# Hyena layer: two pieces of channels in flight, and the short convolution as scaled copies summed by accumulating DMAs

## The chip, the cores and the metric

The kernel runs on one core of a Trainium2 chip. The metric is the device time of one execution in microseconds, as the median of several runs. The five engines have a queue of instructions each, which they work off in order and which wait for one another by semaphores: TensorE (PE, with its weight loads as PEld), VectorE (DVE), ScalarE (ACT), GpSimd (POOL) and SyncE (SP). The last two also issue DMAs.

## The reference

An encoder trunk of two layers on 1024 tokens with 1024 channels: layer 0 mixes by attention and RWKV-7, layer 1 by an order-2 Hyena operator, and both end in a SwiGLU network. The change lies in layer 1's operator:

```
def hyena_mixer(h, w_in, conv_w, conv_b, ..., skip, w_out):
    p = h @ w_in                                  # 1024 -> 3072 channels
    p = conv(p, conv_w, width 3, centred, per channel) + conv_b
    v, x1, x2 = jnp.split(p, 3, axis=-1)
    filt = hyena_filters(...)
    z = v
    for o, gate in enumerate((x1, x2)):
        z = gate * bidirectional_fft_conv(z, filt[:, o, 0], filt[:, o, 1], skip[o])
    return z @ w_out
```

All is in fp32.

## The kernel before, in words

Everything in SBUF lives in pages of 128 partitions by 1024 floats, named `p` in the profile, handed out and taken back in turn; in PSUM there are eight banks (`bk`), in this layer four for the projection (group 0) and four for the convolutions (group 1). A page or bank that is handed out again makes its next writer wait for its last reader.

The projection `p = h @ w_in` makes 24 tiles of 128 channels: 8 for v, 8 for x1, 8 for x2. A tile is 48 matmuls (L296: three products of high and low parts, two halves of the tokens, eight blocks of input channels). The weights of a tile come in two DMAs from GpSimd's queue (L271, `hwi..h` and `hwi..l`), issued one tile ahead. ScalarE then empties the two banks into a padded page (`padded`, L1036), and `hy_short` forms the width-3 convolution: one scaled copy with bias on ScalarE (L1852) and two multiply-adds on VectorE (L1853, L1854). v and x1 tiles are transposed on TensorE (`hy_tok`, L1865) and copied back by ScalarE (L1866). x2 tiles are stored in DRAM (`sp_h`).

Channels are worked in four pieces q of 256, that is two tiles each of v, x1 and x2. Of a piece, `start` makes the first half of a DFT on TensorE (L1804, copied to SBUF at L1805). `hy_conv` does the rest on VectorE: `dft8` (L1654 and L1655), the product with the filter's spectrum, which comes by DMA from `hs` (L1827 to L1832), the first sums of the inverse (L1838, L1839) and another `dft8`. `gate` ends the inverse on TensorE (L1957), multiplies by x1 on VectorE (L1962) and begins the next DFT (`hy_taps`: L1814 on TensorE, L1704 on ScalarE, L1705 and L1706 on VectorE). A second `hy_conv` follows, and `finals` ends the inverse (L1980), multiplies by x2 (L1984) and stores the result (`sp_z`). The pieces run one after another. Under the name `tail` the first four results then go through the first half of the output projection (L256 and L257 split them into high and low parts, L296 multiplies, L787 adds to the residual). The second half (`halves`: L296, L814) follows the stage and ends in the norm before the SwiGLU network.

`weave` interleaves generators of such steps in proportion to quotas: here the chain of pieces (`back`) against the projection followed by `tail` (`rest`). The tile framework then schedules each engine's queue from that program order by its own estimates, so that the order on an engine can differ from that of the code.

Of the kernel before, what the change touches and what calls it, by code (L numbers as in the profile page):

```python
# [12 lines left out]
AF = mybir.ActivationFunctionType  # L13
ALU = mybir.AluOpType
# [7 lines left out]
P = 128  # L22
# [41 lines left out]
def run(gen):  # L64
    for _ in gen:
        pass
# [10 lines left out]
class Kern:  # L77
# [1766 lines left out]
        yield 2.2  # L1844
        return out

    def hy_short(self, pad, j):

        nc = self.nc
        o = self.page()  # L1850
        cw = lambda a: self.c("conv_w", 24 * a + j)
        nc.scalar.activation(out=o, in_=pad[:, 1:1025], func=AF.Identity, scale=cw(1), bias=self.c("conv_b", j))  # L1852
        nc.vector.scalar_tensor_tensor(out=o, in0=pad[:, 0:1024], scalar=cw(0), in1=o, op0=ALU.mult, op1=ALU.add)  # L1853
        nc.vector.scalar_tensor_tensor(out=o, in0=pad[:, 2:1026], scalar=cw(2), in1=o, op0=ALU.mult, op1=ALU.add)  # L1854
        self.free(pad)
        return o
# [13 lines left out]
    def hyena(self, w, h, tail):  # L1870
# [7 lines left out]
        zs = []  # L1878
# [47 lines left out]

        def there(q, n):
            while rs[q].get("n", 0) < n:
                yield

        def Bt(B, t2):
            j, s = self.xpos(t2)
# [3 lines left out]

        def start(q):

            if q < 4:
                yield from there(q, 2)  # L1940
                v = rs[q]["v"]
                st[q] = self.quads(4, 256)
                for t in range(4):
                    self.hy_sums(st[q], v, t, 1)
                    yield 0.1
                self.free(v)

        def gate(q, B):

            x1 = rs[q]["x1"]  # L1950
            s = self.quads(4, 256)
            for i in range(4):
                ps = self.bank(1, (P, 2, 256))
                for j in range(2):
                    t2 = i + 4 * j
                    for ri in range(2):
                        nc.tensor.matmul(ps[:, j], self.G[t2 // 4][:, t2 % 4, 128 * ri : 128 * ri + 128], Bt(B, t2)[:, ri], start=ri == 0, stop=ri == 1)  # L1957
                if i:
                    self.hy_taps(s, x1, i - 1, 1)
                for j in range(2):  # L1960
                    z = x1[j][:, i]
                    nc.vector.tensor_tensor(out=z, in0=z, in1=ps[:, j], op=ALU.mult)  # L1962
                self.fbank(ps)
                yield 0.1
            self.free(B[0])
            self.hy_taps(s, x1, 3, 1)
            self.free(x1)
            yield 0.1
            return s

        def finals(q, B):

            for c in range(2):
                x2 = self.unspill(rs[q]["x2", c])
                for i in range(2):
# [7 lines left out]
                    xv = x2.rearrange("p (a b) -> p b a", b=8)[:, 4 * i : 4 * i + 4]  # L1983
                    nc.vector.tensor_tensor(out=xv, in0=xv, in1=ps, op=ALU.mult)  # L1984
                    self.fbank(ps)
                zs.append(self.spill(x2, f"sp_z{2 * q + c}"))
                self.free(x2)
            self.free(B[0])

        def back():  # L1990
            yield from start(0)
            end = iter(())
            for q in range(4):
                steps = self.hy_conv(st.pop(q), 0, q)
                while True:
                    try:
                        cost = next(steps)
                    except StopIteration as e:
                        B = e.value
                        break  # L2000
                    next(end, None)
                    yield cost
                run(end)
                yield from there(q, 4)
                s = yield from gate(q, B)
                B = yield from self.hy_conv(s, 1, q, start(q + 1))
                yield from there(q, 6)
                end = finals(q, B)
            yield from end

        def rest():
            yield from f
            for a in h:
                self.free(a)
            while len(zs) < 4:
                yield
            for n, _ in enumerate(tail(zs[:4])):
# [7 lines left out]
        return zs[4:]  # L2025


    def final(self, xT, steps, out):
# [182 lines left out]
```

## Time and profile before

| | us |
|---|---|
| median of 3 runs | 3393.94 (3389.41 to 3398.52) |
| the profiled execution | 3396.35 |
| its span | 3394.6 |
| mean granted TensorE clock | 0.958 |
| TensorE busy over the span | 3177.3 (94%) |
| VectorE busy | 2343.3 (69%) |
| ScalarE busy | 1230.9 (36%) |
| GpSimd busy | 197.2 (6%) |

Rows of the profile give a line of the code, the engine, the operation with its tiles, and counts. A row of the order of time begins with start and length in us and ends, in brackets, with the idle time before it and what ended that. Busy time of a matmul includes its pipelined part, so that rows of TensorE overlap a little; the price of one is better taken from the starts of two rows. An fp32 matmul that is not split by the program counts as two instructions in the trace; L296 works on already split parts and counts once. The Hyena stage begins near 2105 us and its last product of a piece ends at 2649 us.

### The profile page before, as it was taken

The page shows a single profiled execution, that of the slowest core. Times are in us where ns is not written, and L with a number is a line of the kernel's source. Part 1 is how long each engine was busy: PE and PEld are TensorE (multiplying, and loading weights), DVE is VectorE, ACT ScalarE, POOL GpSimd, SP SyncE. Part 2 cuts the span into 40 slices and gives each one's busy share as a digit, 9 for nine tenths or more (in the row PEclk, how much of TensorE's full clock was granted, in tenths as well). Part 3 has the DMA queues.
Part 4 walks back from the last instruction along what each step waited for, and adds up shares of the span by engine and source line. Part 5 has one row for each costly group of instructions (what it writes and reads, how often), then busy time and mean ns, then how long its engine had stood idle before and what let it go on. Part 6 is the DMA issues. An engine that isn't in the chain of part 4 may idle for free.

```text
span 3394.6 us, 51189 instructions
## 1 busy us (share of the span) xinstructions
PE 3177.3 (94%) x20227; PEld 2565.5 (76%) x20227; DVE 2343.3 (69%) x4011; ACT 1230.9 (36%) x2146; POOL 197.2 (6%) x443
## 2 busy tenths in 40 slices
PE   8899989988889997999999999989977899999998
PEld 5687767666667886888888887877866788888886
DVE  5465465565766896788877666698997686667545
ACT  4622255455555432532323333222220343333211
POOL 2000000000001110000001210000000000000000
PEclk9999989889999998999999999999988899999999
DMA  7654522333334235244447993323445422224311
GB/s 265 222 174 153 153 71 67 66 98 66 102 68 103 86 137 185 93 158 140 148 148 249 351 317 131 118 89 110 143 167 208 145 81 75 75 93 148 122 47 50
DMA packets 331377, 460.24 MB, mean 136 GB/s; under 512 B 101816, under 2 KB 233745, under 8 KB 331136
## 3 DMA queue, kind: packets, MB, share of 16 engines
q1 hardware_dynamic: 292576, 322.04, 30.9%
q0 software_dynamic: 38384, 134.86, 11.3%
q8 instruction: 159, 2.61, 0.3%
q14 instruction: 82, 0.67, 0.1%
q10 hardware_dynamic: 176, 0.07, 0.0%
HBM read 312.71 MB, written 141.56 MB: 134 GB/s over the span
## 4 chain that ended last, share of the span: by engine, by line
PE 57%; DVE 7%; DMA 5%; issue 4%; ACT 2%; POOL 0%; DVEq 0%; SPq 0%; ACTq 0%; POOLq 0%
PE bk L296 20%; PE bk L600 8%; PE bk L602 8%; PE bk L601 8%; PE bk L1785 3%; DMA p<-in_hy_w_in_dram 2%; DVE p L1654 2%; PE bk L1804 2%; DVE p L257 1%; PE bk L1760 1%; PE bk L1980 1%; PE bk L1332 1%; PE bk L964 1%; PE bk L1814 1%; PE bk L947 1%
## 5 line engine op out<-in xcount | busy, mean ns | idle before, releaser
L296 PE MATMUL bk<-p,p 128*128 128x512 f32 x5136 | 1240.9, 401 | 65.9 <-ACT p L256 31.1
L296 PEld LDWEIGHTS bk<-p,p 128*128 128x128 f32 x5136 | 980.4, 193 | 289.4 <-ACT p L256 34.0
L256 ACT ACTIVATE p<-p 128x512 fp32r<-128x512 f32 (+3 forms) x542 | 403.2, 758 | 946.3 <-PE bk L601 271.2
L257 DVE TENSOR_TENSOR p<-p,p 128x512 fp32r<-128x512 f32 (+3 forms) x542 | 450.8, 847 | 238.7 <-ACT p L256 188.4
L601 PE MATMUL bk<-p,p 128*128 128x512 f32 x1248 | 486.1, 390 | 3.8 <-DVE p L257 3.8
L600 PE MATMUL bk<-p,p 128*128 128x512 f32 x1248 | 485.6, 390 | 0.0
L602 PE MATMUL bk<-p,p 128*128 128x512 f32 x1248 | 485.2, 390 | 0.2 <-DVE p L257 0.2
L601 PEld LDWEIGHTS bk<-p,p 128*128 128x128 f32 x1248 | 234.7, 188 | 53.1 <-DVE p L257 4.7
L602 PEld LDWEIGHTS bk<-p,p 128*128 128x128 f32 x1248 | 234.7, 188 | 49.6 <-DVE p L257 0.6
L600 PEld LDWEIGHTS bk<-p,p 128*128 128x128 f32 x1248 | 234.7, 188 | 48.1
L787 DVE SCALAR_TENSOR_TENSOR p<-bk,mod,p 128x512 f32<-128x512 f32 x192 | 134.8, 744 | 85.5 <-PE bk L296 82.0
L429 DVE SCALAR_TENSOR_TENSOR p<-p,cond,p 128x512 f32<-128x512 f32 x140 | 104.6, 749 | 58.8 <-DMA p<-in_ada_w_dram 56.7
L1785 PE MATMUL bk<-p,p 128*128 128x256 f32 x512 | 127.6, 397 | 6.0 <-DVE p L1706 4.9
L1654 DVE TENSOR_TENSOR p<-p 128x256 f32<-128x256 f32 (+1 forms) x336 | 130.8, 452 | 0.0
L1785 PEld LDWEIGHTS bk<-p,p 128*128 128x128 f32 x512 | 96.7, 197 | 21.0 <-DVE p L1706 6.0
L928 DVE TENSOR_REDUCE mx<-bk 128x1 f32<-128x512 f32 x128 | 86.5, 685 | 36.7 <-PE bk L925 34.8
L1036 ACT COPY p<-bk 128x512 f32<-128x512 f32 (+1 forms) x80 | 43.9, 588 | 182.9 <-DVE p L1831 63.0
L932 ACT ACTIVATE p<-bk,mx 128x512 f32<-128x512 f32 x128 | 87.0, 686 | 51.6 <-DVE mx L929 46.4
L1654 DVE TENSOR_TENSOR p<-p,p 128x1024 f32<-128x1024 f32 (+1 forms) x144 | 91.1, 681 | 18.8 <-ACT p L1805 18.8
L1332 PEld LDWEIGHTS bk<-p,p 64*64 64x64 f32 x2048 | 75.7, 141 | 37.0 <-issue 18.5
L1332 PE MATMUL bk<-p,p 64*64 64x64 f32 x2048 | 88.4, 230 | 16.0 <-DMA p<-o 8.6
L947 PE MATMUL bk<-k_ident,p 128*128 128x128 f32 x512 | 88.4, 302 | 15.5 <-ACT p L932 11.5
(407 smaller groups left out, 4169.9 us busy)
## 6 DMA issues: line engine op xcount, KB each, us to landing
p<-in_ffn_w_dram SPq DMA_DIRECT2D x120, 512.0 KB, 5.3
p<-in_ada_w_dram SPq DMA_DIRECT2D x96, 512.0 KB, 4.6
sp_f<-p POOLq DMA_DIRECT2D x36, 512.0 KB, 5.5
p<-sp_f POOLq DMA_DIRECT2D x36, 512.0 KB, 5.8
hs<-p POOLq DMA_DIRECT2D x32, 512.0 KB, 3.7
p<-hs SPq DMA_DIRECT2D x32, 512.0 KB, 4.5
p<-sp_r SPq DMA_DIRECT2D x24, 512.0 KB, 5.0
p<-sp_x SPq DMA_DIRECT2D x24, 512.0 KB, 4.6
```

What stands on the lines that cost most here:

```text
L256: self.nc.scalar.activation(out=hi, in_=src, func=AF.Copy)
L257: self.nc.vector.tensor_tensor(out=lo, in0=src, in1=hi.bitcast(F32), op=ALU.subtract)
L296: nc.tensor.matmul(ps[n], a, b[:, HALVES[n]], start=s, stop=e)
L429: nc.vector.scalar_tensor_tensor(out=acc, in0=wt[:, i], scalar=self.cond[:, k : k + 1], in1=acc, op0=ALU.mult, op1=ALU.add)
L600: nc.tensor.matmul(ps, op[:, 0, k], mh, start=start and k == 0, stop=False)
L601: nc.tensor.matmul(ps, op[:, 0, k], ml, start=False, stop=False)
L602: nc.tensor.matmul(ps, op[:, 1, k], mh, start=False, stop=stop and k == 3)
L787: nc.vector.scalar_tensor_tensor(out=xs, in0=ps[n], scalar=self.modc(layer, part, m), in1=xs, op0=ALU.mult, op1=ALU.add)
L947: nc.tensor.transpose(pt[:, j], pr[:, k * P : (k + 1) * P], self.ident)
L1332: nc.tensor.matmul(pt[H[p], pr], lhs(e, pr, p), rhs[H[p], 8 * e + pr], start=True, stop=True)
L1654: tt = lambda o, a, b, op: nc.vector.tensor_tensor(out=o, in0=a, in1=b, op=op)
L1785: nc.tensor.matmul(ps[j][:, ri], F[2 * d + t2 // 4][:, t2 % 4, 128 * ri : 128 * ri + 128], tp[:, j, d], start=d == 0, stop=d == 1)
```

## The change

Two things, in one diff.

First, of the 24 projected tiles the four v tiles of pieces 0 and 1 keep the old short convolution. For the other 20, ScalarE makes all three scaled copies, the two outer ones into pages of their own, and two DMAs on GpSimd's queue add these to the first (`accum_op=ALU.add`). The second must wait for the first, because both read and write the same page. The step after the convolution is asked for 8 steps of the projection later instead of 4.

Second, two pieces are in flight: one line of work takes pieces 0 and 2, the other 1 and 3, and both are woven with the projection. The tiles come in the order v, x1, x2 of pieces 0 and 1, then of 2 and 3. The token form of x1 is stored in DRAM (`sp_hx`) and loaded again at the gate. Final products no longer run inside the next piece's first convolution.

```diff
-    def hy_short(self, pad, j):
+    def hy_short(self, pad, j, by_dma):
...
         nc.scalar.activation(out=o, in_=pad[:, 1:1025], func=AF.Identity, scale=cw(1), bias=self.c("conv_b", j))
+        if by_dma:
+            for a in (0, 2):
+                s = self.page()
+                nc.scalar.activation(out=s, in_=pad[:, a : a + 1024], func=AF.Identity, scale=cw(a))
+                nc.gpsimd.dma_start(out=o, in_=s, accum_op=ALU.add)
+                self.free(s)
+            self.free(pad)
+            return o
         nc.vector.scalar_tensor_tensor(out=o, in0=pad[:, 0:1024], scalar=cw(0), in1=o, op0=ALU.mult, op1=ALU.add)
...
-        tiles = [(q, key, c, j + 2 * q + c) for q in range(4) for key, j in (("v", 0), ("x1", 8), ("x2", 16)) for c in range(2)]
+        tiles = [(q, key, c, j + 2 * q + c) for h2 in range(2) for key, j in (("v", 0), ("x1", 8), ("x2", 16)) for q in (2 * h2, 2 * h2 + 1) for c in range(2)]
...
-            o = self.hy_short(pad, j)
-            for _ in range(4):
+            by_dma = key != "v" or q > 1
+            o = self.hy_short(pad, j, by_dma)
+            for _ in range(8 if by_dma else 4):
                 yield
...
                 self.hy_tok(r[key], o, c)
+                if key == "x1" and c == 1:
+                    t = r[key]
+                    flat = lambda a: a.rearrange("p a b -> p (a b)")
+                    r[key] = [self.spill(flat(a), f"sp_hx{q}{n}") for n, a in enumerate(t)]
+                    self.free(t)
...
-            x1 = rs[q]["x1"]
+            x1 = [reshape(self.unspill(d), (P, 4, 256)) for d in rs[q]["x1"]]
...
-        def back():
-            yield from start(0)
...
+        def back(q):
+
+            yield from start(q)
+            B = yield from self.hy_conv(st.pop(q), 0, q)
+            yield from there(q, 4)
+            s = yield from gate(q, B)
+            B = yield from self.hy_conv(s, 1, q)
+            yield from there(q, 6)
+            yield from finals(q, B)
+
+        def line(h2):
+
+            for q in (h2, 2 + h2):
+                yield from back(q)
...
-        weave((335, back()), (267, rest()))
+        weave((168, line(0)), (168, line(1)), (300, rest()))
```

In the changed kernel lines from 1857 on have new numbers: the accumulating DMA is L1857, the two outer copies L1856, the multiply-adds L1861 and L1862, the transposes L1873 with their copies L1874, the gate's matmul L1970 and product L1975, the final matmul L1993 and product L1997. Lines before 1847 keep theirs.

How the queues change, at three places. On GpSimd's queue before, where the projection is at the first x1 tiles, there are only the weights of coming tiles and the zeros of the padded pages (L1033, L1034):

```order
L271 DMA p_238<-hwi10h 128x1024 [waits DMASW5_49,PE_49]
L271 DMA p_10858<-hwi10l 128x1024 [waits DMASW6_49,PE_49]
L271 DMA p_10846<-hwi11h 128x1024 [waits DMASW7_49,PE_49]
L271 DMA p_10874<-hwi11l 128x1024 [waits DMASW0_49,PE_49]
L1033 MEMSET p_16085 128x1 [waits DVE_49,Activation_49]
```

and now (`DMASW` is a wait for a DMA of this queue):

```order
L1857 DMA p_86<-p_106 128x1024 [waits DMAHW7_49,Activation_49]
L1033 MEMSET p_94 128x1 [waits Pool_49]
L1034 MEMSET p_94 128x1 [waits Activation_49]
L1857 DMA p_86<-p_126 128x1024 [waits DMASW7_49]
L1033 MEMSET p_16057 128x1 [waits DMAHW6_49,DVE_49]
L271 DMA p_10846<-hwi11h 128x1024 [waits DMASW3_49,PE_49]
L271 DMA p_10874<-hwi11l 128x1024 [waits DMASW4_49,PE_49]
```

Between two pairs of weights there now stands a pair of accumulations, of which the second waits for the first.

On SP's queue before, around the first gate, the spectra (`hs`, L1827) and the stores of x2 (`sp_h`) alternate, and x1 does not appear:

```order
L1827 DMA p_16041<-hs_9434 128x1024 [waits DVE_49,Activation_49]
L206 DMA sp_h_16683<-p_16053 128x1024 [waits DMASW2_49,DMAHW1_49,DVE_49,Activation_49]
L206 DMA sp_h_16772<-p_102 128x1024 [waits DMAHW2_49,DVE_49]
L1827 DMA p_106<-hs_10347 128x1024 [waits DMAHW6_49,DVE_49,PE_49]
L1827 DMA p_16041<-hs_10347 128x1024 [waits DMAHW0_49,DMAHW4_49,DVE_49,PE_49]
```

and now:

```order
L206 DMA sp_hx_16823<-p_16045 128x1024 [waits DMAHW4_49,Activation_49]
L206 DMA sp_hx_16825<-p_16081 128x1024 [waits DMAHW7_49,DMAHW5_49,Activation_49]
L1827 DMA p_16081<-hs_9720 128x1024 [waits DMAHW6_49,DMAHW5_49]
L206 DMA sp_h_17168<-p_86 128x1024 [waits DMASW0_49,Pool_49]
L211 DMA p_126<-sp_hx_16823 128x1024 [waits DMAHW4_49,DVE_49]
L211 DMA p_90<-sp_hx_16825 128x1024 [waits DMAHW1_49,DVE_49]
```

The loads of x1 for the first gate stand behind the store of the first x2 tile, which waits for that tile's accumulations.

On VectorE's queue before, behind the last gate, the spectral products of one piece follow one another (`L1838` and `L1839` are its next sums):

```order
L1831 TENSOR_TENSOR p_16061<-p_16053 128x2x256
L1832 TENSOR_TENSOR p_16061<-p_16045 128x2x256
L1831 TENSOR_TENSOR p_16069<-p_16057 128x2x256
L1832 TENSOR_TENSOR p_16069<-p_106 128x2x256
L1655 SCALAR_TENSOR_TENSOR p_130<-p_114,p_16077 128x256 x2
L1655 SCALAR_TENSOR_TENSOR p_94<-p_114,p_16077 128x512 x2
L1655 SCALAR_TENSOR_TENSOR p_130<-p_114,p_16077 128x256 x2
L1838 TENSOR_TENSOR p_90<-p_16061 128x512
```

and now:

```order
L1655 SCALAR_TENSOR_TENSOR p_130<-p_114,p_16057 128x256 x2
L1838 TENSOR_TENSOR p_16065<-p_16053 128x512
L1838 TENSOR_TENSOR p_102<-p_90 128x512
L1838 TENSOR_TENSOR p_102<-p_16073 128x512
L1839 TENSOR_TENSOR p_86<-p_16073 128x512
L1828 TENSOR_TENSOR p_16057<-p_16085,p_16069 128x512
L1828 TENSOR_TENSOR p_94<-p_16049,p_16081 128x512
L1829 TENSOR_TENSOR p_94<-p_16049,p_16081 128x512
L1829 TENSOR_TENSOR p_16057<-p_16085,p_16069 128x512
L1828 TENSOR_TENSOR p_16053<-p_130,p_16045 128x512
```

Sums of the one piece (L1838, L1839) now stand ahead of spectral products of the other (L1828, L1829): behind the last gate two pieces are on their way to the end.

More of the change, by code (lines that the diff above doesn't have):

```diff
@@ L1928, in there @@
             while rs[q].get("n", 0) < n:
-                yield
+                yield "wait"
         def Bt(B, t2):
@@ L1937, in start @@
         def start(q):
[L1939 to L1946, printed above, removed]
+            yield from there(q, 2)
+            v = rs[q]["v"]
+            st[q] = self.quads(4, 256)
+            for t in range(4):
+                self.hy_sums(st[q], v, t, 1)
+                yield 0.5
+            self.free(v)
         def gate(q, B):
-            x1 = rs[q]["x1"]
+            x1 = [reshape(self.unspill(d), (P, 4, 256)) for d in rs[q]["x1"]]
             s = self.quads(4, 256)
@@ L1985, in finals @@
                     self.fbank(ps)
-                zs.append(self.spill(x2, f"sp_z{2 * q + c}"))
+                zs[2 * q + c] = self.spill(x2, f"sp_z{2 * q + c}")
                 self.free(x2)
             self.free(B[0])
-        def back():
-            yield from start(0)
[L1992 to L2009, printed above, removed]
+        def back(q):
[9 more added lines that the diff above has]
+                yield from back(q)
         def rest():
@@ L2015, in rest @@
             while len(zs) < 4:
-                yield
-            for n, _ in enumerate(tail(zs[:4])):
+                yield "wait"
+            for n, _ in enumerate(tail([zs[i] for i in range(4)])):
                 yield 1.0 if n == 0 else 5.3
```

4 lines of the change are left out of this document (2 added, 2 removed).

## The prediction

> **What bounds the stage now.** I read the windows first, to see which engine carries the Hyena stage, then the chain of waits of TensorE inside it, then the order of time for the price of each kind of work. The span is 3394.6 us, the profiled execution 3396.35 us, 2.4 us above the median of the runs shown (3393.94), so I work in the trace and subtract 2.4 at the end.
>
> The windows, core 0: length, then busy time of TensorE, of its weight loads, of VectorE, ScalarE and GpSimd with instruction counts, then the granted clock, the DMA share and GB/s.
>
> ```profile
> 2108.70:2590.50 481.80, 443.31 (x2042) 371.51 (x2042) 402.88 (x695) 99.82 (x149) 29.26 (x78) 0.95 0.39 130
> 2594.50:2649.00 54.50, 29.75 (x121) 24.37 (x122) 51.28 (x92) 1.06 (x1) 3.18 (x6) 0.72 0.60 199
> 2296.00:2321.00 25.00, 25.00 (x112) 20.75 (x111) 24.96 (x41) 2.33 (x3) 2.41 (x7) 1.00 0.43 155
> ```
>
> From the third projection to the last gate, TensorE is busy 92% and VectorE 84%: both are near full, and neither alone sets the time. In the last 54.5 us VectorE is busy 94%, and TensorE waits at a clock of 0.72: there VectorE sets it.
>
> What TensorE waited for between 2108.7 and 2590.5 (total us, times, longest), then the rows at the borders of these windows:
>
> ```profile
> PE bk L1865 <- ACT p L1036: 16.9, 4, 5.8
> PE bk L296 <- ACT p L256: 12.4, 2, 7.9
> PE bk L296 <- ACT p L1866: 5.3, 3, 4.5
> PE bk L1814 <- DVE p L1706: 1.8, 3, 0.6
> PE bk L1814 <- DVE p L1962: 1.4, 1, 1.4
> PE bk L1804 <- ACT p L1866: 0.5, 2, 0.3
> ...
> 2108.70 8.95 PE L296 MATMUL bk<-p,p 128*128 128x512 f32 x27 [4.28 <-DMA p<-hwi8h]
> 2589.82 1.02 PE L1814 MATMUL bk<-p,p 128*128 128x256 f32 x4
> 2590.50 3.80 PE L296 MATMUL bk<-p,p 128*128 128x512 f32 x15
> 2593.89 0.68 DVE L1706 SCALAR_TENSOR_TENSOR p<-p,bk 128x512 f32<-128x512 f32 x1
> 2644.59 4.39 DVE L1984 TENSOR_TENSOR p<-p,bk 128x512 f32<-128x512 f32 x4 [3.17 <-PE bk L1980]
> ```
>
> The idle time is 481.8 - 443.3 = 38.5 us. The five rows other than L256 sum to 25.9: they lie around the gates, where one piece has nothing for VectorE until its gate is through. The L256 row (12.4) is the output projection that waits for the first pieces.
>
> **TensorE's floor.** Prices at full clock, from starts in the order of time:
>
> ```profile
> 2117.48 1.06 PE L1865 MATMUL bk<-k_ident,p 128*128 128x128 f32 x8
> 2118.30 10.50 PE L296 MATMUL bk<-p,p 128*128 128x512 f32 x45
> ...
> 2257.32 7.07 PE L1804 MATMUL bk<-p,p 128*128 128x256 f32 x32
> 2264.04 0.81 PE L296 MATMUL bk<-p,p 128*128 128x512 f32 x2
> ...
> 2281.20 5.52 PE L1980 MATMUL bk<-p,p 128*128 128x128 f32 x48
> 2286.56 0.27 PE L1865 MATMUL bk<-k_ident,p 128*128 128x128 f32 x1
> 2286.59 33.61 PE L296 MATMUL bk<-p,p 128*128 128x512 f32 x147
> 2320.04 1.89 PE L1957 MATMUL bk<-p,p 128*128 128x256 f32 x8
> 2321.58 4.94 PE L296 MATMUL bk<-p,p 128*128 128x512 f32 x20
> ```
>
> L296: 33.45/147 = 0.2276 us. L1804: 6.72/32 = 0.21. L1980: 5.36/48 = 0.1117. L1957: 1.54/8 = 0.1925, and L1814, of the same shape, alike. Transposes: 0.82/8 = 0.1025. An fp32 product counts as two instructions in the trace. Up to the last L1814, before issues 1209 L296, 128 transposes, 256 L1804, 128 each of L1957 and L1814, 192 L1980: 275.1 + 13.1 + 53.8 + 49.3 + 21.4 = 412.7. So 481.8 holds 69.1 beyond the floor: 38.5 idle and 30.6 of matmuls at less than full clock. After issues 1213 L296 and 128 L1980 there, the rest alike: 406.5.
>
> **The parts of the change.**
>
> *Short convolution of 20 tiles.* Forty VectorE operations go, forty ScalarE operations and forty DMAs on GpSimd's queue come:
>
> ```profile
> L1854 DVE SCALAR_TENSOR_TENSOR p<-p,cols,p x24: 1266/1277/1285, 2108.7 to 2532.9; 128x1024 f32<-128x1024 f32 x24
> L1852 ACT ACTIVATE p<-p,cols x24: 1237/1246/1262, 2105.0 to 2528.5; 128x1024 f32<-128x1024 f32 x24
> 2123.16 1.08 ACT L1036 COPY p<-bk 128x512 f32<-128x512 f32 x2 [3.96 <-PE bk L296]
> 2195.75 0.75 DVE L1962 TENSOR_TENSOR p<-p,bk 128x256 f32<-128x256 f32 x2 [0.38 <-PE bk L1957]
> 2303.04 0.53 POOL L271 DMA_DIRECT2D p<-hwi12h  x1 [9.81 <-PE bk L296]
> 2303.56 0.54 POOL L271 DMA_DIRECT2D p<-hwi12l  x1
> ```
>
> VectorE loses 40 x 1.28 = 51 us of 403. That is no gain by itself, because TensorE's 406.5 stand above it; it makes room for two pieces. ScalarE gains 40 x 1.25 = 50 on 99.8 in 481.8: hidden, at about a third busy. GpSimd's queue gains 40 x 0.53 = 21 on 29: hidden as issue time. Its waits are another matter: the second accumulation of a tile waits on that queue for the first, and the weight loads (L271) stand behind. A tile's projection is 48 L296, 11 us, and a load may be one tile late in the queue before TensorE misses it.
>
> *The latency D of an accumulating DMA* is not in this trace. The nearest rows:
>
> ```profile
> hs<-p POOLq DMA_DIRECT2D x32, 512.0 KB, 3.7
> sp_x<-p SPq DMA_DIRECT2D x16, 256.0 KB, 2.0
> sp_h<-p SPq DMA_DIRECT2D x8, 512.0 KB, 4.1
> p<-sp_h SPq DMA_DIRECT2D x8, 512.0 KB, 3.6
> hwi5l<-p POOLq DMA_DIRECT2D x1, 512.0 KB, 10.1
> ```
>
> If the extra read of the destination is free, D is 3.7. If it is serial, 512 KB more cost twice (4.1 - 2.0), so D is 7.9. Beside a crowd of transfers it is 10.1 + 4.2 = 14.3 at worst. I take 5.8, midway between the first two, since the stage's DMA share is only 0.39.
>
> How much may D be? The x1 loads of a gate stand on SP's queue behind the spill of the first x2 tile, which waits for both its accumulations. From the end of that tile's projection to the gate's first L1814 there stand on TensorE 71 L296 (16.2), 16 L1957 (3.1) and 16 transposes (1.6): 20.9 us. The path is 3.6 on ScalarE (both evacuations, 1.08, and two scaled copies of 1.25), 2D, 3.6 for the load and 0.7 for the products (L1962): it fits while D is under 6.5. Above that each us of D costs 2 us at each of four gates. At 5.8 it costs nothing.
>
> *Two pieces in flight.* The DVE order lets one piece's DFT and spectral products run while the other passes its gate, so part of the 25.9 us of waits goes. I take half, 13.0: with 51 us less on VectorE (about 330 us of work before the last gate instead of 403) either piece mostly has something ready, but ScalarE's evacuations still wait for pages that now also hang on DMAs. The L256 waits (12.4) go: at the projection's place all four first pieces have been stored long before. The slow-clock time I scale with the waits: 30.6 x 13.0/38.5 = 10.3. So up to the last gate: 406.5 + 13.0 + 10.3 = 429.8, against 481.8: **52.0 less.** What ends last there is TensorE's own queue.
>
> The start is as before: VectorE's first DFT waits for the first piece's 64 L1804, which stand at the same place. The new quotas of the weaving and the order of the 24 tiles act only through the order counted here.
>
> *x1 through DRAM* adds 8 stores and 8 loads of 512 KB on SP's queue. They are hidden (3.6 to 4.1 us each, DMA share 0.39) except through the path above.
>
> *The tail* gets longer, because two pieces now end together. Prices:
>
> ```profile
> 2619.14 1.28 DVE L1828 TENSOR_TENSOR p<-p,p 128x512 f32<-128x512 f32 x2
> 2621.55 1.40 DVE L787 SCALAR_TENSOR_TENSOR p<-bk,mod,p 128x512 f32<-128x512 f32 x2
> 2622.87 2.34 DVE L1830 TENSOR_TENSOR p<-p,p 128x1024 f32<-128x1024 f32 x2
> 2629.95 2.35 DVE L1654 TENSOR_TENSOR p<-p,p 128x1024 f32<-128x1024 f32 x2
> ...
> 2638.79 2.62 DVE L1655 SCALAR_TENSOR_TENSOR p<-p,p 128x256 f32<-128x256 f32 x6
> ```
>
> Behind the last gate VectorE has three DFTs instead of two, five spectral products instead of four, 13 sums instead of 8 and 8 final products instead of 4. A DFT is 2629.95 to 2641.41 = 11.46; a spectral product 4 x 0.64 + 1.17 = 3.73; five sums 3.2; four finals 4.4; two L787 and one L257 fewer save 1.4 + 1.2. That is 11.46 + 3.73 + 3.2 + 4.4 - 2.6 = **20.2 more**. TensorE has 33 L296 (7.5 us) to do there: no cover. The second half of the output projection then has 24 L296 behind the tail that stood in its waits before (5.5), and two more splits behind the last finals (L257, of L1830's size: 2 x 1.17 = 2.3): **7.8 more**.
>
> The sum: 52.0 - 20.2 - 7.8 = 24.0 less. 3396.35 - 24.0 = 3372.3, less 2.4: **3370 us**.
>
> **A rule that speaks against it.** The row at 2303.04 is a GpSimd DMA issue of 0.53 us inside a stretch in which VectorE was busy 24.96 of 25.00 us, and it was followed 0.52 us later by the next issue. The Trainium skill, page "SBUF — State Buffer", section "Who interferes with whom", says that a DMA issued by GpSimd can stall because a VectorE operation in a two-port mode keeps GpSimd from writing descriptors. By that rule forty more such DMAs beside a busy VectorE would be the new bottleneck; the trace speaks against it here, and the same page says that tensor_tensor has no such mode.
>
> **Rivals.**
>
> 1. *The gates' waits stay* (ScalarE's evacuation waits for a page, now of either piece). Then 25.9 idle and 30.6 x 25.9/38.5 = 20.6 slow clock remain: 453.0, 28.8 less, against 28.0 more behind it. 3393 us, no change. For it: the largest row, L1865 behind L1036, is such a wait. Against it: 51 us less on VectorE, which frees those pages.
> 2. *Accumulation latency on the gates' path: slower.* At D = 12 it costs 4 x 2 x (12 - 6.5) = 44: 3414 us. The gain is gone at 6.5 + 24/8 = 9.5. For it: the 10.1 row and in-order queues on SP, GpSimd and ScalarE. Against it: a free DMA share of 0.6.
> 3. *VectorE starves descriptor writing: slower.* If each of the 40 DMAs waited half of a 25 us stretch, 500 us would be added, near 3870. Nearly excluded by the issue row above.
> 4. *All waits and all slow clock go:* 406.5, so 75.3 less and 28.0 more: 3347 us.
>
> **Chances and range.** The forecast 0.53, rival 1 0.19, rival 2 and other slower mixes of it 0.21, rival 3 0.02, rival 4 0.05. The median's bound for telling a change is 0.3%, 10.2 us. Faster: 0.53 + 0.05 = 0.58, of which 0.02 falls back to no change at the forecast's edge. The range runs from rival 4's side, 3348, to rival 2, 3414; with all 69.1 us of loss kept and the longer tail it would be 3415. The forecast's own range is 3352 to 3384.
>
> **What would show it.** L1861 has 4 instructions instead of 24; L1857 lands in under 6.5 us. TensorE's idle time before the last L1814 is near 13 us and no L256 wait stands in it. Between the last L1706 and the last final product (L1997) lie about 75 us instead of 54.5. I am wrong if L1857 lands in 9 us or more, if L296 waits for weights, or if L1814 or L1970 waits for the x1 loads.

## The result, and the profile after

The changed kernel takes 3440.57 us (median of 4 runs, 3433.61 to 3448.39) against 3396.23 us of the kernel before on the same chip: ratio 1.0127, 95% interval 1.0111 to 1.0143. It is slower by 44 us, and outside the range. Its profiled execution (3440.21 us, span 3438.4) is near that median.

Where the 43.8 us between the two spans lie, by landmarks in the order of time:

| stretch | before | after | difference | forecast |
|---|---|---|---|---|
| start of the stage (first scaled copy, L1852) | 2104.95 | 2106.71 | +1.8 | 0 |
| from there to the end of the last L1814 | 485.9 | 504.8 | +18.9 | -52.0 |
| to the end of the last L1706 | 3.7 | 1.9 | -1.8 | |
| tail: to the last final product (L1984, now L1997) | 54.4 | 76.0 | +21.6 | +20.2 |
| to the start of the last row of L450 (second half of the output projection) | 58.0 | 62.7 | +4.7 | +7.8 |
| the rest | | | -1.4 | |

The tail came as forecast. The stretch ahead of the last gate did not: it was to become 52 us shorter and became 19 longer.

The windows of the changed kernel: the stage up to the last gate, the tail, the second half of the output projection (columns as in the prediction).

```profile
2110.50:2611.50 501.00, 437.78 (x1984) 364.75 (x1985) 337.17 (x617) 141.15 (x189) 65.71 (x120) 0.93 0.63 176
2613.50:2689.50 76.00, 24.53 (x153) 22.70 (x151) 70.49 (x128) 0.00 (x0) 3.17 (x6) 0.66 0.55 190
2689.50:2752.20 62.70, 58.24 (x256) 48.34 (x257) 38.08 (x58) 26.69 (x43) 0.00 (x0) 0.95 0.45 162
```

VectorE has indeed 66 us less to do before the last gate (402.88 in the row of before, 337.17 here), and TensorE's busy time fell by 6. But TensorE is idle for 63.2 us (501.0 - 437.8; 38.5 before), and the DMA share rose from 0.39 to 0.63. What TensorE waited for in that stretch (total us, times, longest; the wait for the weights hwi2h, at its start, was there before as well, for hwi8h):

```profile
PE bk L296 <- ACT p L1036: 15.4, 2, 14.5
PE bk L296 <- ACT p L256: 12.3, 1, 12.3
PE bk L1970 <- DVE p L1655: 8.0, 1, 8.0
PE bk L1814 <- DVE p L1975: 5.5, 1, 5.5
PE bk L296 <- ACT p L1874: 4.5, 2, 4.0
PE bk L296 <- DMA p<-hwi2h: 4.4, 1, 4.4
PE bk L1873 <- ACT p L1036: 4.3, 1, 4.3
PE bk L1814 <- ACT p L1704: 4.1, 1, 4.1
```

The waits behind evacuations (L1036) are 19.7 us, little more than the 16.9 before. What grew is the waits of the gates' own matmuls: 3.2 us before (L1814), 24.3 now (L1970 and L1814, with three more rows of 3.4, 1.8 and 1.5 us).

The longest wait, in the order of time: TensorE waits for a bank, ScalarE's evacuation of that bank (L1036) waits for a page, and the page is still in use by an accumulation (`p<-p`). On GpSimd's queue the first of that tile's pair waits for ScalarE, and the second for the first.

```profile
2333.65 3.11 PE L296 MATMUL bk<-p,p 128*128 128x512 f32 x13
2351.29 2.07 PE L296 MATMUL bk<-p,p 128*128 128x512 f32 x4 [14.53 <-ACT p L1036]
...
2335.94 1.24 ACT L1852 ACTIVATE p<-p,cols 128x1024 f32<-128x1024 f32 x1 [2.99 <-DVE p L1706]
2350.65 1.07 ACT L1036 COPY p<-bk 128x512 f32<-128x512 f32 x2 [13.47 <-DMA p<-p]
...
2337.75 0.89 POOL L1857 DMA_DIRECT2D p<-p  x1 [11.98 <-ACT p L1852]
2343.91 0.89 POOL L1857 DMA_DIRECT2D p<-p  x1 [4.19 <-DMA p<-p]
```

The DMAs' median landing in us: the accumulation is what the prediction took (5.8), but the stores of x2 and the loads of the spectra, which took 4.1 and 4.5 before, are slower. The stores of x1 (`sp_hx`) are new.

```profile
p<-p POOLq DMA_DIRECT2D x40, 512.0 KB, 5.8
p<-hs SPq DMA_DIRECT2D x32, 512.0 KB, 5.4
sp_hx<-p SPq DMA_DIRECT2D x8, 512.0 KB, 9.3
sp_h<-p SPq DMA_DIRECT2D x8, 512.0 KB, 9.2
```

In the tail TensorE waits for VectorE, now for two pieces:

```profile
2653.81 3.48 PE L1993 MATMUL bk<-p,p 128*128 128x128 f32 x16 [34.74 <-DVE p L1654]
2672.22 9.62 PE L1993 MATMUL bk<-p,p 128*128 128x128 f32 x62 [14.93 <-DVE p L1655]
```

### The profile page after: what moved, and what is told of

The parts are those of the page before. It is cut to its first block, busy times and chain, and to the rows that moved or that the text cites. A ratio compares the mean times of both kernels' runs of the same rounds, so it can differ in the third digit from the quotient of the medians.

```text
span 3438.4 us, 51309 instructions
## 1 busy us (share of the span) xinstructions
PE 3164.6 (92%) x20227; PEld 2556.9 (74%) x20227; DVE 2297.3 (67%) x3971; ACT 1272.9 (37%) x2188; POOL 233.3 (7%) x483
## 3 DMA queue, kind: packets, MB, share of 16 engines
q1 hardware_dynamic: 294880, 330.43, 31.1%
q0 software_dynamic: 44144, 155.83, 14.7%
## 5 line engine op out<-in xcount | busy, mean ns | idle before, releaser
L296 PE MATMUL bk<-p,p 128*128 128x512 f32 x5136 | 1236.7, 400 | 71.4 <-ACT p L256 36.2
L296 PEld LDWEIGHTS bk<-p,p 128*128 128x128 f32 x5136 | 976.5, 192 | 290.6 <-ACT p L256 38.4
L256 ACT ACTIVATE p<-p 128x512 fp32r<-128x512 f32 (+3 forms) x542 | 401.8, 758 | 944.8 <-PE bk L601 248.1
L601 PEld LDWEIGHTS bk<-p,p 128*128 128x128 f32 x1248 | 234.3, 188 | 52.2 <-DVE p L257 4.2
L1654 DVE TENSOR_TENSOR p<-p 128x256 f32<-128x256 f32 (+1 forms) x336 | 132.3, 451 | 13.8 <-DMA p<-p 5.9
L1654 DVE TENSOR_TENSOR p<-p,p 128x1024 f32<-128x1024 f32 (+1 forms) x144 | 91.1, 679 | 37.7 <-ACT p L1805 33.1
L1785 PEld LDWEIGHTS bk<-p,p 128*128 128x128 f32 x512 | 97.6, 199 | 19.6 <-DVE p L1706 4.3
L947 PE MATMUL bk<-k_ident,p 128*128 128x128 f32 x512 | 86.6, 297 | 16.9 <-ACT p L932 12.8
L1036 ACT COPY p<-bk 128x512 f32<-128x512 f32 (+1 forms) x80 | 43.7, 588 | 156.3 <-PE bk L296 57.2
```

Of the source, the lines that this page charges most:

```text
L256: self.nc.scalar.activation(out=hi, in_=src, func=AF.Copy)
L296: nc.tensor.matmul(ps[n], a, b[:, HALVES[n]], start=s, stop=e)
L601: nc.tensor.matmul(ps, op[:, 0, k], ml, start=False, stop=False)
L1654: tt = lambda o, a, b, op: nc.vector.tensor_tensor(out=o, in0=a, in1=b, op=op)
L1785: nc.tensor.matmul(ps[j][:, ri], F[2 * d + t2 // 4][:, t2 % 4, 128 * ri : 128 * ri + 128], tp[:, j, d], start=d == 0, stop=d == 1)
```

## The experiments

Theory A: the accumulating DMAs cost the time, by their own duration, the queues or the pages that they hold. Theory B: two pieces in flight are themselves the cost. All results in one table. "Stretch" runs from the first L1852 to the end of the last L1814, "tail" from the last L1706 to the last final product, both in the profiled execution; that lies up to some 10 us off the median (18 above it for the later step). Each ratio is to the kernel before on the same chip, where its median was 3392.6 to 3396.2; two kernels of different chips are better compared by their ratios, each of which is known to about 0.2 to 0.3% (5 to 11 us).

| kernel | median us | ratio to before (95%) | stretch | tail |
|---|---|---|---|---|
| before, 26 pages | 3396 | | 485.9 | 54.4 |
| changed, 26 pages | 3440.57 | 1.0127 (1.0111 to 1.0143) | 504.8 | 76.0 |
| two pieces only | 3413.03 | 1.0060 (1.0038 to 1.0082) | 485.3 | 72.5 |
| DMAs only | 3415.08 | 1.0055 (1.0034 to 1.0075) | 500.9 | 52.8 |
| one DMA for each tile | 3411.92 | 1.0057 (1.0035 to 1.0078) | 481.3 | 72.3 |
| DMAs copy, do not add | 3417.07 | 1.0067 (1.0049 to 1.0085) | 480.5 | 76.8 |
| two pieces only, uneven lines | 3415.33 | 1.0060 (1.0039 to 1.0081) | 504.8 | 52.2 |
| later step (16) | 3467.87 | 1.0228 (1.0195 to 1.0260) | 549.9 | 72.0 |
| DMAs for x2 only | 3422.59 | 1.0087 (1.0067 to 1.0108) | 491.9 | 75.9 |
| stores on GpSimd's queue | 3433.05 | 1.0111 (1.0089 to 1.0134) | 500.6 | 75.7 |
| changed, 27 pages | 3436.21 | 1.0139 (1.0105 to 1.0172) | 503.7 | 72.7 |
| changed, 28 pages | 3418.08 | 1.0070 (1.0053 to 1.0086) | 486.9 | 78.6 |
| two pieces only, 27 pages | 3408.69 | 1.0042 (1.0023 to 1.0062) | 478.0 | 73.1 |
| two pieces only, 28 pages | 3400.64 | 1.0020 (1.0006 to 1.0033) | 466.7 | 79.2 |
| before, 23 pages | 3412.79 | 1.0052 (1.0037 to 1.0067) | 498.5 | 56.1 |
| before, 27 pages | 3406.03 | 1.0036 (1.0020 to 1.0052) | 495.5 | 56.6 |
| before, 28 pages | 3413.75 | 1.0048 (1.0031 to 1.0065) | 501.1 | 54.9 |
| two pieces only, uneven (200 to 136), 28 pages | 3391.81 | 1.0000 (0.9985 to 1.0015) | 491.1 | 52.3 |
| the same with the DMAs | 3431.93 | 1.0122 (1.0088 to 1.0155) | 525.8 | 53.7 |
| two pieces only, uneven (188 to 148), 28 pages | 3404.30 | 1.0027 (1.0012 to 1.0042) | 495.2 | 53.0 |

### Each part of the change alone

Two pieces in flight, without the DMAs:

```diff
-            by_dma = key != "v" or q > 1
+            by_dma = False
```

> Two pieces in flight, all 24 short convolutions on VectorE. Theory A (the accumulating DMAs and the pages they hold make the 94 us of loss before the last gate): the stage up to the last gate falls from 500.7 us to 455 or less and the time to 3396 or less, the tail stays near 77 us. Theory B (two pieces in flight are themselves the cost: longer tail, gates of both pieces at the same time, x1 through DRAM): the stage stays at 490 or more, since VectorE also gets 51 us back, and the time stays at 3430 or more.

This edit also brings the step behind the convolution back from 8 to 4, and it keeps x1's way through DRAM and the new order of the tiles; no run separates these from the second piece.

The DMAs without the second piece: the kernel before, with the changed `hy_short` and the 8 steps behind it.

```diff
-            o = self.hy_short(pad, j)
-            for _ in range(4):
+            by_dma = key != "v" or q > 1
+            o = self.hy_short(pad, j, by_dma)
+            for _ in range(8 if by_dma else 4):
```

> The pieces one after another as before, the short convolution of 20 tiles by ScalarE and accumulating DMAs. Theory A: TensorE waits more at the gates than the 25.9 us of before, the time is 3415 or more, the tail stays at 54.5 us. Theory B: VectorE's 51 us less or the DMAs' latency change little, 3380 to 3400, and the tail stays at 54.5 us.

Neither theory holds alone. Two pieces cost 17 us (3413.03), all of it behind the gate: the tail is 18 us longer and the stretch ahead of it is unchanged, 485.3. The DMAs cost 19 us (3415.08), and in the profile it is ahead of the last L1814: stretch +15, tail -1.6. The two costs add up to 36 of the 44. With the DMAs only, the loss is not at the gates: what grew most is the wait of the output projection (12.4 before):

```profile
PE bk L296 <- ACT p L256: 27.2, 1, 27.2
```

The waits of TensorE with two pieces only, up to the last gate:

```profile
PE bk L1873 <- ACT p L1036: 15.0, 2, 8.3
PE bk L1970 <- DVE p L1655: 8.8, 2, 8.2
PE bk L296 <- ACT p L256: 6.1, 1, 6.1
```

The gates' waits did not go when a second piece was there to fill them: TensorE's idle time in this stretch, counted as above, is 39.0 us (38.5 before). The waits are again for an evacuation, and now also of a gate's matmul for VectorE.

### What of an accumulating DMA costs

One of the two outer copies on VectorE again:

```diff
-            for a in (0, 2):
+            nc.vector.scalar_tensor_tensor(out=o, in0=pad[:, 0:1024], scalar=cw(0), in1=o, op0=ALU.mult, op1=ALU.add)
+            for a in (2,):
```

> As the changed kernel, but of the two outer copies only one comes by an accumulating DMA; the other is a multiply-add on VectorE (20 x 1.28 = 26 us more there). Theory A: the chain of a tile is one DMA shorter (5.8 us and its wait on GpSimd's queue), the waits fall by half or more of the excess: 3415 or less. Theory B: within 10 us of the changed kernel, 3430 to 3450.

The same DMAs without the addition:

```diff
-                nc.gpsimd.dma_start(out=o, in_=s, accum_op=ALU.add)
+                nc.gpsimd.dma_start(out=o, in_=s)
```

> As the changed kernel, but the 40 DMAs copy instead of adding, so the two outer taps are not summed. Tells what the adding itself costs. Theory A in the form that the adding makes the DMA slow: landing falls from 5.8 to about 3.7 us as for the nearest plain row, and the time to 3420 or less. Theory A in the form that any DMA there holds pages and queues: landing 4.5 us or more, time 3430 or more. Theory B: 3430 or more whatever the landing.

With one DMA for each tile the time is that of two pieces without any (3411.92 against 3413.03), and 28.7 us less than with two for each tile (24 by the ratios). Part of that difference can be order, since the scheduler writes another one for each of these three kernels. The copying DMAs are the cleanest pair, because the five engines have the very same order of instructions as in the changed kernel, and only the sums are left out: the addition alone costs 23.5 us (3440.57 - 3417.07; 20 by the ratios), and the stretch is 24.4 us longer with it. TensorE is idle for 43.6 us with copies and for 63.2 with the addition.

The longest wait shown above is not part of that cost, for it is nearly as long with copies (14.53 with the addition):

```profile
2339.33 2.93 PE L296 MATMUL bk<-p,p 128*128 128x512 f32 x6 [13.96 <-ACT p L1036]
```

The 24 us come up in several smaller steps, above all where in the changed kernel L1873 waits 4.3 us (0 with copies), one L1814 4.1 (0), L1970 8.0 (2.5) and the output projection 12.3 (8.9), and in slow matmuls behind these waits.

The rows on L1857 in the changed kernel (duration of the issue; DMAs that waited for it or were waited for; landing):

```profile
L1857 POOL DMA_DIRECT2D p<-p x40: 860/886/923, 2165.3 to 2546.0; - x40
...
  POOL p L1857: 83.5, 16
  ACT p L1036: 50.4, 4
  POOL p L1033: 20.7, 4
...
DMA to landing us min/median/max: 4.5/5.8/12.7
```

and with plain copies:

```profile
L1857 POOL DMA_DIRECT2D p<-p x40: 527/530/560, 2166.8 to 2521.2; - x40
...
  POOL p L1857: 55.8, 15
  ACT p L1036: 27.0, 3
  POOL p L1033: 14.9, 4
...
DMA to landing us min/median/max: 2.8/4.2/12.0
```

1.6 us more of landing for each goes with 23.4 us more of ScalarE's evacuations waiting for such a page, and 27.7 us more of second accumulations waiting for the first. Other writers wait for such pages too, L1704 on ScalarE (13.5 us, 7.5 with copies) and L1654 and L1828 on VectorE (10.1 and 12.2; 2.9 and 8.6). All such waits of the two engines up to the last gate are 97 us with the addition and 48 with copies: in one and the same order, the addition mainly costs by holding pages longer. The queue of GpSimd's DMAs (packets, MB, share of the 16 DMA engines' span) shows what the addition does to the engines. Before, changed, plain copies:

```profile
q0 software_dynamic: 38384, 134.86, 11.3%
```

```profile
q0 software_dynamic: 44144, 155.83, 14.7%
```

```profile
q0 software_dynamic: 44144, 155.83, 12.9%
```

11.3% of 3394.6 us are 383.6, 14.7% of 3438.4 are 505.4, 12.9% of 3416.4 are 440.7. If the rest of the queue took what it did before, 40 plain copies took all 16 engines 57 us, 1.4 us each, and 40 accumulations 122 us, 3.0 us each: about twice as long. The Trainium skill, page "DMA: Bandwidth & Descriptors", section "Rules for kernel authors", says that an accumulate reads its destination and writes it later; a second stream of reads agrees with the doubled time, though these runs do not show what the engines do in it.

### Is it the place in the queues?

```diff
-            for _ in range(8 if by_dma else 4):
+            for _ in range(16 if by_dma else 4):
```

> The changed kernel, but the step behind the short convolution (transposes, stores) is asked for 16 steps of the projection later instead of 8. Theory A1 (the latency of the accumulations reaches TensorE because the transposes and x1 loads stand too early in the queues): the waits shrink, the stretch up to the last gate falls from 504.8 us to 485 or less, the time to 3420 or less. Theory A2 (pages held by the accumulations are what is missing; a later step holds them longer): the evacuation's waits for a page grow beyond 50 us and the time stays at 3435 or more.

```diff
-            by_dma = key != "v" or q > 1
+            by_dma = key == "x2"
```

> The changed kernel, but only the eight x2 tiles by accumulating DMAs (16 DMAs instead of 40); nothing of x2 passes TensorE before the final products. Theory A1 (latency on the way to transposes and x1 loads): about as the kernel with two pieces and no such DMA, 3405 to 3418, or better by VectorE's 20 us. Theory A2 (pages and queues shared by all): in proportion to the DMAs, 3413 + 0.4 x 27 = 3424 or more.

Here the other tiles' step goes back from 8 to 4.

```diff
-                r[key, c] = self.spill(o, f"sp_h{2 * q + c}")
+                r[key, c] = self.spill(o, f"sp_h{2 * q + c}", nc.gpsimd)
...
-                    r[key] = [self.spill(flat(a), f"sp_hx{q}{n}") for n, a in enumerate(t)]
+                    r[key] = [self.spill(flat(a), f"sp_hx{q}{n}", nc.gpsimd) for n, a in enumerate(t)]
```

> The changed kernel, but the stores of x1 and x2 go on GpSimd's queue instead of SP's, so that the loads of spectra and of x1 no longer stand behind stores that wait for accumulations. Theory A3 (SP's queue in order is the cost): VectorE's waits for the spectra (31.8 us) and for x1 (13.0) nearly vanish, the landing of the spectra falls from 5.4 to about 4, the time to 3425 or less. Theories A1 and A2: 3435 or more, and more still if the weights of the projection now come late behind the stores.

The later step, which should have given the latency more room, makes it 27 us worse, so A1's forecast failed; but a later step also puts the gates later, so this run does not price the latency by itself. A2 had the time right and not the reason: the evacuations waited only 7.4 us for accumulations (and 16.1 for a store of x1), and TensorE waited 22.4 us before L1970 for VectorE's L1654 instead of 1.8. The DMAs for x2 alone, which TensorE never waits for directly, cost 9.6 us over none, just under what A2 gave them (3424): near the share of 16 in 40 (11), as a cost that all tiles share would be. Moving the stores off SP's queue gives back 7.5 us by the medians, which is not clear of noise (the intervals overlap) and less than A3 asked. Of the waits that it should have removed (28.2 and 13.0 us in the changed kernel) most stay:

```profile
DVE p L1828 <- DMA p<-hs: 26.6, 11, 5.9
DVE p L1975 <- DMA p<-sp_hx: 13.9, 5, 5.4
```

So A3, the path on which the prediction had put its threshold, is the smaller part. The same section of the Trainium skill's page says that spreading DMAs over issuing engines only saves issue time, since all run on the same 16 DMA engines; a gain of 7.5 us at most agrees.

### Pages

The list of free pages, counted in the program's order of the stage each time that a page is handed out, holds 12.2 on average before (least 6), 11.6 with the DMAs only (6), 9.5 with two pieces only (4), and 8.9 in the changed kernel (1). The fewer are free, the sooner a page goes to its next writer.

```diff
-    K.repage(26, 20)
+    K.repage(28, 20)
```

> The changed kernel with 28 pages in place of 26 for this layer. Counted in the program's order, the list of free pages holds 8.9 on average when a page is handed out (12.2 in the kernel before, least 1 against 6); two more pages make that about 10.9. Page theory (a page comes back to its next writer before its last reader, often a DMA, is done): ScalarE's evacuations (L1036) wait less than half of 50.4 us for accumulations, the stretch up to the last gate falls from 504.8 us to 490 or less, the time to 3425 or less. Rival (the order on TensorE and the chains of two pieces set it, pages are a symptom): 3435 or more.

> Two pieces in flight, short convolution all on VectorE, 28 pages instead of 26 (mean free 9.5 becomes about 11.5). Page theory: the 15 us that the transposes wait for the evacuation go, 3400 or less against 3413. Rival: 3408 or more.

> The kernel before with 28 pages instead of 26 (mean free 12.2 becomes about 14.2). Page theory: the 16.9 us that the transposes wait for the evacuation at the gates shrink; 3375 to 3390. Rival (those waits come from the order of work, not from pages): 3392 to 3400.

The opposite, 23 pages in the kernel before:

> The kernel before with 23 pages instead of 26 (mean free 12.2 becomes about 9.2, as in the changed kernel, least 3). Page theory: it loses as the two pieces in flight do before the last gate, 3405 or more. Rival: within 8 us of 3396.

Both kernels with two pieces gain from pages: 22.5 us and 12.4 us with 28. The stretch of the changed kernel falls to 486.9, and its evacuations wait 30.8 us for accumulations instead of 50.4; the page theory had asked for under 25.2. With two pieces only, the wait that should have gone did not: the transposes waited 15.0 us for the evacuation and still wait 15.6. And the kernel before loses by two more pages, 18 us, which the page theory cannot explain. Its waits with 28 pages:

```profile
PE bk L1865 <- ACT p L1036: 26.8, 3, 13.7
PE bk L1865 <- DVE p L1854: 13.6, 1, 13.6
```

The number of pages also changes the order that the framework's scheduler writes, on every engine, and here the transposes came to stand ahead of work that was not ready (these two rows are 40.4 us; the transposes waited 16.9 with 26 pages). Is the kernel before with 26 pages a lucky order, then, and the 44 us an accident? The same three with 27:

> The kernel before with 27 pages instead of 26. Theory O (the kernel before stands on an order that happens to be good, and any other order costs 10 to 20 us): 3405 to 3418, as with 23 and 28. Theory N (28 was an exception): 3390 to 3400.

> The changed kernel with 27 pages instead of 26. Page theory: between the two known points, 3418 to 3441, near 3429. Theory O alone (every order of it is a draw): anywhere from 3410 to 3445, not ordered by the pages.

> Two pieces in flight, short convolution all on VectorE, 27 pages. Page theory: between 3401 and 3413, near 3407. Theory O alone: 3395 to 3425.

Partly. With 26, 27 and 28 pages the kernel before takes 3396, 3406, 3414; two pieces only 3413, 3409, 3401; the changed one 3441, 3436, 3418. The accumulating DMAs, with the step of 8 that comes with them, cost 27.5, 27.5 and 17.4 us over two pieces only, so in each of three orders. Two pieces alone cost +17, +3 and -13 against the kernel before with as many pages: that part of the loss depends on the pages and on the order, and is not a property of having two pieces. How much of it is order and how much pages stays open, since no run changed the one without the other.

With 28 pages and no DMAs the second piece does part of what the prediction wanted from it: the stretch is 466.7 us, 19 less than in the kernel before with 26 pages, and TensorE is idle for 31.1 us of it (38.5). The tail of 79.2, 25 us longer, takes that back.

### The tail

```diff
-        weave((168, line(0)), (168, line(1)), (300, rest()))
+        weave((200, line(0)), (136, line(1)), (300, rest()))
```

> Two pieces in flight with the short convolution all on VectorE, and the two lines woven 200 to 136 instead of 168 to 168, so that only one piece is left behind the last gate (two DFTs and four spectral products, as before). Theory A (the 20 us of tail come from two pieces ending together): the tail falls from 72.5 us to 52 to 56; the stretch up to the last gate takes up part of it, since that work now lies ahead of the gate: 485 to 500 us, the time 3395 to 3412 against 3413 of the even lines. Theory B (the tail is set by something else, such as the loads of x2 or TensorE's clock): the tail stays above 65 us.

The windows up to the last gate and behind it:

```profile
2099.32:2604.11 504.79, 449.12 (x2080) 375.89 (x2080) 409.03 (x702) 102.07 (x152) 33.69 (x89) 0.95 0.46 156
2606.05:2658.29 52.24, 22.96 (x97) 19.45 (x98) 49.10 (x88) 2.35 (x3) 0.00 (x0) 0.61 0.28 96
```

The tail falls by 20.2 us to about what it was before, as theory A said, but the stretch grows by 19.5, more than it allowed, and the time stays: VectorE's work only moved from one side of the gate to the other (409.0 us ahead of it against 386.7). With 28 pages the trade is better:

> Two pieces in flight, short convolution all on VectorE, lines woven 200 to 136, 28 pages. If the work only moves from behind the gate to ahead of it, as it did with 26 pages: tail near 54 us, the stretch before it longer by about as much, 3398 to 3405. If TensorE's idle time can take it up now that pages are there: 3375 to 3390, and faster than the kernel before.

The stretch is 491.1 there, and the time, 3391.81, is that of the kernel before (1.0000), between the two ranges expected. It is the best version found with two pieces, and not faster. The accumulating DMAs in it, and another weaving:

> The changed kernel with lines woven 200 to 136 and 28 pages, that is the best version so far plus the accumulating DMAs. If these cost what they did with even lines (17 to 28 us): 3409 to 3420. If pages enough and a short tail hide them: 3388 to 3398; if VectorE's 51 us less tell at last: below 3385.

> Two pieces in flight, short convolution on VectorE, 28 pages, lines woven 188 to 148. One piece is left behind the last gate, as with 200 to 136, so the tail is 52 to 56 us. If the order is only a draw: 3385 to 3410; if nearer to even is better ahead of the gate: below 3390.

In their fourth pair the DMAs cost 40 us, more than expected. The weaving of 188 to 148 has the short tail too and takes 3404: within what a draw of the order allows, and nearer to even is not better. No version beat the kernel before.

## Why the prediction was wrong

**The step that failed is the one up to the last gate:** "I take half, 13.0" for the waits, none for the output projection, and 10.3 for the slow clock, 23.3 together. Measured by the same floor (406.5): 63.2 us idle, of which 12.3 are the output projection (L296 behind L256), and 437.8 - 406.5 = 31.3 of matmuls above the floor, 94.5 together. The difference, 71 us, is as large as the whole error (3440.57 - 3370 = 70.6); the small errors of the other terms cancel. Neither half of the change did what this step asked: the second piece alone left the idle time as it was (39.0), and the DMAs raised it, by 4.6 us where they only copy (in another order) and by another 19.6 where they add (in the same one).

- *Waits.* The argument was that at the gates one piece "has nothing for VectorE", and that VectorE's relief and a second piece give either piece something to do. VectorE was relieved, by 66 us, and it shows little: copying DMAs, which relieve it as much, leave the stretch 4.8 us shorter than two pieces without DMAs (480.5 against 485.3; what the copies themselves cost is not separated). What TensorE waited for in the rows of before was an evacuation without a page (L1865 behind L1036, 16.9), and the evacuations waited above all for pages that VectorE's spectral products still read, so at those times VectorE had work and no page came free:

```profile
ACT p L1036 <- DVE p L1831: 63.0, 5, 13.9
```

  A second piece takes pages, and so do the scaled copies. Rival 1 had this mechanism; it was priced as if the pages' waits could only stay as they were.
- *Latency D.* The value was right, 5.8, the median of 40, partly by luck: it was the middle of two bounds, 3.7 and 7.9, and the plain DMA here takes 4.2. "At 5.8 it costs nothing" was wrong: the addition, which moves D from 4.2 to 5.8, costs 24 us in the same order of instructions. The threshold of 6.5 stood on one path (x2's store ahead of x1's load on SP's queue), and moving that store off the queue gave back 7.5 us at most. The paths left out were the page of each copy until its DMA has landed (shown by the waits above), and the second accumulation behind the first ahead of weights and clears (L1033) on GpSimd's queue. The longer engine time may also slow the other transfers: the loads of the spectra land in 5.4 us against 4.9 with copies, the stores of x1 in 9.3 against 6.2 (medians of 32 and 8). The median also hid landings of up to 12.7.
- *Slow clock.* The term was read wrongly and scaled wrongly. The trace grants TensorE a clock of either 1.00 or 0.50 in this stretch. One of the stretches at half clock in the changed kernel (length, TensorE busy, clock, DMA share, GB/s), then the sums of all seven before and of all eight now:

```profile
2339.44:2356.51 17.07, 5.22 (x12) 0.50 0.73 200
sum 51.20, PE 38.03; mean PE 5.43
sum 68.26, PE 34.73; mean PE 4.34
```

  At half clock, 38.0 and 34.7 busy us lose 19.0 and 17.4 us. So of the 30.6 and 31.3 us above the floor 11.6 and 13.9 are not clock, and what they are stays open. Nor does the loss follow the idle time (38.5 and 63.2 us). The Trainium skill, page "TensorE: Matmul & The Clock Gate", section "Part 1: The HAM clock gate (the "warmup" mystery)", says that an idle window of about 3.4 us halves the clock and a busy one of that length restores it. By that rule the loss goes by the number of long waits, not by their length, because a slow clock costs nothing while TensorE stands still. The trace agrees: the stretches at half clock are multiples of 3.41 us, and waits of over 4 us number 7 before and 8 now.
- *The output projection's wait* was said to go, since the first pieces would long be stored. It stayed at 12.3 (12.4 before; 6.1 with two pieces only, 27.2 with the DMAs only). The last of the first four stores is issued at 2439.93, but the loads stand on SP's queue between other work, the second of them behind the store of an x2 tile, and such stores wait for accumulations:

```profile
2439.93 0.32 SPq L206 DMA_DIRECT2D sp_z<-p  x1
...
2541.97 0.32 SPq L211 DMA_DIRECT2D p<-sp_z  x1
2550.57 0.32 SPq L206 DMA_DIRECT2D sp_h<-p  x1
2551.06 0.32 SPq L211 DMA_DIRECT2D p<-sp_z  x1
```

- *The tail* was right: +20.2 forecast, +21.6 measured, and the uneven lines took it back to 52.2. What the prediction did not see is that shortening it again moves the work ahead of the gate, where nothing takes it up.
- *The second half of the output projection*: +7.8 forecast, +4.7 measured.
- *Rival 2* has the right sign and, for the DMAs' part, the right operation, but the wrong mechanism: not D = 12 on one path, but D = 5.8 on several.
- *Rival 3* is out: L1857 issues in 0.886 us against 0.530 for the plain copy beside the same VectorE work, so that even this excess belongs to the addition and not to VectorE.
- *Of the signs named,* L1861 with 4 instructions, landing under 6.5 us and a tail of about 75 us came; idle time near 13 us and no wait behind L256 did not. One of the signs of being wrong came too, one step removed: L1814 waited 5.5 us for the product L1975, which itself waited 13.0 us for x1's loads.

## What to carry to other kernels

Where two engines are each near full, as TensorE (92%) and VectorE (84%) were here, 66 us less work on one of them did not shorten the stage: look first at what the other waits for. Here it waited for work that had no free buffer. Before giving a second unit of work a price, count the free buffers in program order, and each new holder with the time until its DMA has landed; and ask what happens when two units end together, for that cost 18 to 25 us of tail. In one order of instructions, letting 40 DMAs add instead of copy cost 24 us, at a landing only 1.6 us longer. A kernel whose order a scheduler writes can move by 10 to 18 us when only its number of buffers changes, so a loss of that size needs a second order of the same work before it is laid to a mechanism.

## What the runs showed of the hardware that was not expected

- An accumulating SBUF-to-SBUF DMA of 512 KB takes the 16 DMA engines about 3.0 us, a plain one 1.4 (by the shares of queue q0 above), and lands in 5.8 against 4.2 us (medians of 40).
- Its issue on GpSimd takes 0.886 us against 0.530, and issues of weights (L271) right behind it take as long, 0.88 and 0.89 us at 2338.30 and 2338.83, where those at 2323.91 and 2325.24, ahead of it, took 0.54 and 0.53:

```profile
2323.91 0.54 POOL L271 DMA_DIRECT2D p<-hwi7h  x1 [10.01 <-PE bk L296]
2325.24 0.53 POOL L271 DMA_DIRECT2D p<-hwi7l  x1 [0.79 <-PE bk L296]
2337.75 0.89 POOL L1857 DMA_DIRECT2D p<-p  x1 [11.98 <-ACT p L1852]
2338.30 0.88 POOL L271 DMA_DIRECT2D p<-hwi12h  x1
2338.83 0.89 POOL L271 DMA_DIRECT2D p<-hwi12l  x1
```

  With starts 0.53 to 0.55 us apart they overlap in the record, so that the queue itself goes on at the old pace.
